# A streaming encoder layer on one core: the recurrence moved, in half chunks, beside the paired projection products, and the window it had taken away

## The chip, the cores and the metric

The kernel runs on one core of a Trainium2 chip. The metric is the device time of one execution in microseconds (us), the median of several runs. The engines are TensorE (PE; its weight loads are listed apart as PEld), VectorE (DVE), ScalarE (ACT), GpSimd (POOL) and the queue that issues every DMA (SP).

## The reference

One layer for 1152 tokens: 1024 of a prompt and 8 x 16 of samples that continue from caches. From `u`, the normalised input, one projection gives eleven blocks of 1024 columns. Three branches use them, and a gated sum merges them:

```python
q, k, v, g_a, x_r, g_b, q_m, g_c, g_m = split(u @ w_in)
A: o_a = diff_attention(q, k, v) * silu(g_a)        # 8 heads, samples see 512 cached tokens
B: x_c = conv_b + sum(xpad[:, j:j+T] * conv_w[j])   # causal, width 4
   r, i = sigmoid(x_c @ rg_wa + rg_ba), sigmoid(x_c @ rg_wx + rg_bx)   # 8 diagonal blocks of 128
   a = exp(-8 * r * softplus(-rg_lambda));  b = sqrt(1 - a*a) * (i * x_c)
   h[t] = a[t] * h[t-1] + b[t];   o_b = h * silu(g_b)
C: o_c = cross_attention(q_m, memory of 256 tokens, 4 heads) * silu(g_c)
m = sum_i sigmoid(g_m[i]) * (o_i @ w_branch[i]);  y = LayerNorm(alpha * u + m @ w_o)
```

## The kernel before

All large products are made in three TensorE passes over a high and a low part (`mm3`, L142), and everything is held transposed: 128 channels on the partitions, the 1152 tokens along the free axis. `uhi` and `ulo` (8 channel blocks x 1152 tokens) are the moving operand of every projection and, later, of every merge: they hold `u` first and then one branch output after the other.

A **chunk** is 128 output columns of a weight matrix. `units_for` (L457) makes it in three **units** of 384 tokens, each of 24 matmuls, and loads the weights two chunks ahead. `gm_units` (L478) makes a chunk of merge gate `g_m` (a tanh on ACT, then a store to `d_gm`). `m_units(i, e)` (L488) makes chunk `e` of the merge of branch `i` (A is 0, B 1, C 2): it loads the gate (`gmr`) and, except for the first branch, the running sum (`mr`), combines them on DVE and stores the sum to `d_m`.

The body runs **windows** one after the other (L1404), each with its own SBUF pool and its own PSUM banks:

- a (L526): prompt self-attention with its own chunks, then one chunk of `g_m`
- s (L800): sample self-attention, with 6 chunks of `g_m` (18 units) put between its steps
- p (L1070): sums and differences of quarters of `u` (`piece`, L1076), with 3 chunks of `g_m`. A last set of five pieces overwrites one quarter of `uhi`/`ulo`
- g (L1145): the other 46 chunks of the projection, in 23 pairs (`jobs`)
- b (L1300): the recurrence of branch B, with A's merge (24 units) as filling
- c (L704): prompt cross-attention, with 9 units of B's merge
- x (L951): sample cross-attention, with the other 15 units of B's merge

C's merge, the output product and the final LayerNorm follow. Two functions put a branch output back into `uhi`/`ulo`: `o_get` (L509) loads it from `d_oT`, and `o_put` (L514) splits it with a cast on ACT and a subtraction on DVE.

A **job** of window g makes two chunks with seven products of half the depth and half the tokens instead of eight. `step(i, j)` (L1238) is product `j` of job `i`: 24 matmuls of 288 tokens, two halves of 12. Three accumulators, X, Z and Y, of two PSUM banks each, rotate from job to job:

```python
mov = [B11, T3, 1, B21, 0, B22, 2]
role = ["X", "Z", "X", "Y", "X", "X", "Z"]
```

X takes products 0, 2, 4 and 5, and it is read out after each of them, so the readout of one half must be over before the next product's matmuls of that half. `g_prep(q + 3)` (L1113) makes the weights of a product three products ahead: on DVE the sums, then a cast on ACT and a subtraction on DVE. The banks of Z of one job are those of Y in the next. A job that makes `x_r` ends in the convolution (`Conv.done`, L1184: eight DVE instructions); one that makes a gate ends in a tanh on ACT and a product on DVE.

Window b takes the 8 channel blocks one after the other, in five steps for each: the gates of three stretches of 384 tokens (six groups of three matmuls, tanh on ACT), `rec1` (L1328: exponential, tanh and square root on ACT, a product on POOL, two on DVE), `rec2` (L1342: the scan over all 1152 tokens on DVE) and `rec3` (L1356). The split input `xhl` and the gate tile `t` have one buffer each. Its order is written out as

```python
wk.seq = [setup] + weave(fill[:20], at) + fill[20:23] + [lambda: put(0), fill[23], lambda: put(1), lambda: put(2)]
```

`weave` spreads one list evenly over another. This is the order in which instructions are asked for; a list scheduler then gives each engine its queue, in which an instruction that it reckons to be ready may stand ahead of one asked for earlier. On the chip every engine, and SP, works through its queue in order.

Of the kernel before, what the change touches and what calls it, by code (L numbers as in the profile page):

```python
# [18 lines left out]
D = 1024  # L19
# [15 lines left out]
GM_T = (1, 6, 3)  # L35
# [83 lines left out]
def body(tc, A):  # L119
# [355 lines left out]
    gmp = pool(left, "gmp", 4)  # L475
    gm_next = [0]

    def gm_units(stop=False):  # L478
# [3 lines left out]
        def ev(c, t):  # L482
            g = gmp.tile([128, TC], F32, name="gms", tag="gms")
            SC.activation(g, t, AF.Tanh, scale=0.5)
            SY.dma_start(d_gm[i][:, TC * c:TC * c + TC], g)
        return units_for(COL_GM + 128 * i, ev, stop=stop)

    def m_units(i, e, put=None, stop=False):  # L488
        x = {}

        def pre(c):
            x["g"] = gmp.tile([128, TC], F32, name="gmr", tag="gms")
            SY.dma_start(x["g"], d_gm[8 * i + e][:, TC * c:TC * c + TC])
            if i:
                x["m"] = gmp.tile([128, TC], F32, name="mr", tag="ms", bufs=3)
                SY.dma_start(x["m"], d_m[e][:, TC * c:TC * c + TC])

        def ev(c, t):
# [5 lines left out]
            if i:  # L504
                V.tensor_tensor(g, x["m"], g, OP.add)
# [12 lines left out]
    def gate_ev(G):  # L518
        def ev(c, t):
            g = gmp.tile([128, TC], F32, name="gts", tag="gms")  # L520
# [183 lines left out]
    def window_c():  # L704
# [88 lines left out]
        for e in range(3):  # L793
            fill += m_units(1, e)
# [5 lines left out]
    def window_s():  # L800
# [112 lines left out]
        def fin2(g):  # L913
# [10 lines left out]
            if g == 1:  # L924
                SY.dma_start(d_oT[0].rearrange("h p t -> p h t")[:, :, S:T], X["oT"])
# [25 lines left out]
    def window_x():  # L951
# [93 lines left out]
        for e in range(3, 8):  # L1045
            fill += m_units(1, e)
# [21 lines left out]


    def window_p():  # L1070
# [5 lines left out]
        def piece(c, n, last):  # L1076
            q = {}
            need = ((0, 1), (1, 1)) if last else ((0, 0), (0, 1), (1, 0), (1, 1))
            for k, t in need:
# [3 lines left out]
            if last:  # L1083
                sub(y[0], q[1, 1], q[0, 1])
                a = (slice(None), slice(0, 4), slice(TH + c, TH + c + n))
                split(uhi[a], ulo[a], y[0])
                return
# [6 lines left out]
        cs = [(128 * j, 128) for j in range(4)] + [(512, 64)]  # L1094
        fill = []
        for j in range(GM_T[2]):
            fill += gm_units(stop=j == GM_T[2] - 1)
        a = [lambda c=c: piece(*c, False) for c in cs]
        wk.seq = weave(fill, a) + [lambda: (g_load(0), g_load(1), g_prep(0))]
        wk.seq += [lambda c=c: piece(*c, True) for c in cs]  # L1100
# [12 lines left out]
    def g_prep(q):  # L1113
# [7 lines left out]
        elif j == 1:  # L1121
            a = tmp("s3")
            sub(a, quad(0, 0), quad(1, 0))
# [5 lines left out]
        elif j == 3:  # L1129
            a = quad(0, 1)  # L1130
# [405 lines left out]
```

## Time and profile before

| | us |
|---|---|
| median of 3 runs (2023.32 to 2025.5) | 2025.39 |
| the profiled execution | 2022.76 |
| its span, first to last instruction | 2021.0 |
| PE busy in the span | 1948.7 |
| DVE busy | 1229.9 |
| ACT busy | 851.1 |
| POOL busy | 104.6 |

The span is what the rows below divide; the profiled execution is 1.8 us longer than its span. PE's busy time is modelled, since matmuls overlap: two matmuls of 384 tokens are each listed with about 0.34 us, though in a row one starts every 0.174 us. So PE's real time is read from where instructions start, or from a run of equal ones, not from the busy column.

### The profile page before, as it was taken

To read this page: it belongs to the slowest core of one execution; us is meant where nothing else is said; L and a number is where in the kernel's file an instruction comes from. 1 tells how busy PE (TensorE), PEld (TensorE's weight loads), DVE (VectorE), ACT (ScalarE), POOL (GpSimd) and SP (SyncE) were. 2 spreads that over 40 slices of the span, in tenths; PEclk is the share of its full clock that TensorE was granted. 3 is DMA by queue.
4 is the path that set the end of the run, shared out by engine and by line. 5 is a ranking of instruction groups with operands and counts; after the bars stand their busy time and mean duration, and the time that the engine had idled before them with its cause. 6 is when DMAs were issued, how large, how long until landed. Compare 5 with 4: busy or idle time off the path is not lost.

```text
span 2021.0 us, 34019 instructions
## 1 busy us (share of the span) xinstructions
PE 1948.7 (96%) x13424; PEld 1827.6 (90%) x13424; DVE 1229.9 (61%) x2404; ACT 851.1 (42%) x1725; POOL 104.6 (5%) x178
## 2 busy tenths in 40 slices
PE   7999999999999999999999999999999499999998
PEld 7999999999999876799999999999999398889986
DVE  7731787667786444446554565555667675454397
ACT  5432566555665333333333333434666452232120
POOL 2100000000000011000000000000011101000000
PEclk9999999999999999999999999999999699999999
DMA  8753122211221487664223222333876486895332
GB/s 271 247 147 101 40 71 67 78 55 53 63 67 58 141 285 238 189 189 131 95 97 116 100 101 90 110 100 112 268 231 208 164 294 223 285 302 174 102 126 94
DMA packets 291487, 297.36 MB, mean 147 GB/s; under 512 B 17332, under 2 KB 255028, under 8 KB 291328
## 3 DMA queue, kind: packets, MB, share of 16 engines
q1 hardware_dynamic: 291328, 295.20, 45.6%
q8 instruction: 105, 1.72, 0.4%
q14 instruction: 54, 0.44, 0.1%
HBM read 209.54 MB, written 85.61 MB: 146 GB/s over the span
## 4 chain that ended last, share of the span: by engine, by line
PE 83%; DMA 5%; DVE 5%; ACT 3%; issue 2%; SPq 1%; POOL 0%; DVEq 0%; ACTq 0%; POOLq 0%
PE pj L140 39%; PE ba L1261 8%; PE bb L1261 8%; PE bc L1261 8%; PE sc L140 7%; PE o L140 5%; PE tr L641 2%; PE tr L855 1%; DMA ocr<-d_oT 1%; PE pv L140 1%; ACT K L567 1%; DMA uq<-d_u 1%; DVE t L1352 1%; PE tr L982 1%; DMA xc<-d_xc 1%
## 5 line engine op out<-in xcount | busy, mean ns | idle before, releaser
L140 PE MATMUL pj<-uhi,xh 128*128 128x384 f32 x1392 | 477.9, 343 | 2.1 <-DVE soT L921 1.5
L140 PE MATMUL pj<-uhi,xl 128*128 128x384 f32 x1392 | 474.4, 341 | 0.0
L140 PE MATMUL pj<-ulo,xh 128*128 128x384 f32 x1392 | 472.9, 340 | 0.6 <-DVE ulo L133 0.6
L140 PEld LDWEIGHTS pj<-uhi,xh 128*128 128x128 f32 x1392 | 263.1, 189 | 11.2 <-issue 9.1
L140 PEld LDWEIGHTS pj<-uhi,xl 128*128 128x128 f32 x1392 | 262.9, 189 | 7.1 <-issue 6.1
L140 PEld LDWEIGHTS pj<-ulo,xh 128*128 128x128 f32 x1392 | 263.0, 189 | 6.4 <-issue 5.3
L136 ACT CAST xh<-xr 128x512 fp32r<-128x512 f32 x150 | 90.0, 618 | 177.0 <-PE pj L140 103.8
L623 ACT ACTIVATE p<-p,sst 128x256 f32<-128x256 f32 (+6 forms) x128 | 100.6, 786 | 17.7 <-DVE sst L620 16.3
L140 PE MATMUL pj<-w,uhi 128*128 128x256 f32 x576 | 106.9, 285 | 0.5 <-ACT uhi L136 0.2
L133 DVE TENSOR_TENSOR xl<-xr,xh 128x512 fp32r<-128x512 f32 x116 | 78.9, 685 | 44.3 <-ACT xh L136 44.0
L140 PE MATMUL pj<-wo,mh 128*128 128x512 f32 x432 | 98.6, 390 | 0.4 <-ACT wo L136 0.4
L620 DVE CUSTOM_DVE_ANT_0 p<-sc,th 128x256 f32<-128x256 f32 (+6 forms) x128 | 96.5, 768 | 3.1 <-PE sc L140 2.0
L140 PEld LDWEIGHTS pj<-wo,mh 128*128 128x128 f32 x432 | 80.8, 188 | 17.9 <-ACT wo L136 1.1
L140 PE MATMUL sc<-K,Q 128*128 128x512 f32 (+4 forms) x384 | 94.5, 356 | 0.0
L140 PEld LDWEIGHTS pj<-w,uhi 128*128 128x128 f32 x576 | 90.5, 191 | 1.6 <-ACT uhi L136 0.9
L500 DVE SCALAR_TENSOR_TENSOR gmr<-gmr,pj 128x384 f32<-128x384 f32 x72 | 39.6, 550 | 81.0 <-PE pj L140 80.9
L140 PE MATMUL pj<-w,ulo 128*128 128x256 f32 x288 | 82.2, 286 | 1.7 <-DVE ulo L133 1.6
L140 PE MATMUL o<-v,wT 128*128 128x128 f32 x576 | 80.2, 278 | 0.0
L140 PEld LDWEIGHTS o<-v,wT 128*128 128x128 f32 x576 | 74.2, 192 | 3.4 <-ACT wT L169 1.5
L551 DVE SCALAR_TENSOR_TENSOR Q<-pj,Q 64x384 fp32r<-64x384 f32 (+1 forms) x48 | 24.5, 511 | 79.7 <-ACT Q L550 79.2
L140 PEld LDWEIGHTS sc<-K,Q 128*128 128x128 f32 x384 | 63.9, 189 | 3.8 <-DVE sst L620 1.5
L567 ACT CAST K<-kr 64x384 fp32r<-64x384 f32 (+1 forms) x96 | 45.7, 476 | 48.4 <-DVE kr L562 47.2
(314 smaller groups left out, 4055.2 us busy)
## 6 DMA issues: line engine op xcount, KB each, us to landing
xr<-in_w_in_dram SPq DMA_DIRECT2D x80, 512.0 KB, 4.0
ck<-in_cache_k_dram SPq DMA_DIRECT2D x32, 512.0 KB, 4.9
cv<-in_cache_v_dram SPq DMA_DIRECT2D x16, 1024.0 KB, 5.5
gmr<-d_gm SPq DMA_DIRECT2D x72, 192.0 KB, 3.3
xr<-in_w_branch_dram SPq DMA_DIRECT2D x24, 512.0 KB, 4.9
ocr<-d_oT SPq DMA_DIRECT2D x32, 384.0 KB, 5.0
d_m<-gmr SPq DMA_DIRECT2D x48, 192.0 KB, 3.3
mr<-d_m SPq DMA_DIRECT2D x48, 192.0 KB, 4.3
```

What stands on the lines that cost most here:

```text
L133: V.tensor_tensor(out, a, b, OP.subtract)
L136: SC.copy(hi, src)
L140: PE.matmul(out, a, b, start=start, stop=stop)
L500: V.scalar_tensor_tensor(g, g, 1.0, t, op0=OP.add, op1=OP.mult)
L551: V.scalar_tensor_tensor(q[b], t[a, :n], -1.0, raw(q[a]), op0=OP.mult, op1=OP.subtract)
L567: SC.copy(kh[b], kr[a, :n])
L620: V.tensor_tensor_reduce(s[:, :L].rearrange("p (a b) -> p a b", a=nb), ps[z][:, :nb, :w], X["th"][:, 896 - 128 * i:896 - 128 * i + L].rear ...
L623: SC.activation(s[:, :L], s[:, :L], AF.Exp, scale=-1.0, bias=st_[:, z, i:i + 1], accum_out=st_[:, 2 + z, i:i + 1])
L641: PE.transpose(t[:, 128 * j:128 * j + 128], X["w", h, i][:, 128 * k:128 * k + 128], ident)
L855: PE.transpose(t[:, 128 * j:128 * j + 128], X["ck", n, s // 2][:, j, 128 * (s % 2):128 * (s % 2) + 128], ident)
L982: PE.transpose(t[:, 256 * d + 128 * m:256 * d + 128 * m + 128], X["k", b][:, m, c:c + 128], ident)
L1261: PE.matmul(t, w[:, p, k, :], m[v][:, k, a], start=first and k == 0 and y == 0, stop=last and k == 3 and y == 2, skip_group_check=True)
```

## The change

The windows are now a, p, g, s, c, x; window b is gone.

- The recurrence runs in window g, in 16 halves (8 blocks x 2 halves of 576 tokens), seven steps each, woven between the products from job 8 to the last but one. The carry from one half to the next is the column `hc`. Its gates use two more PSUM banks (`tr`).
- Window s has B's merge (24 units) in place of 6 chunks of gates. Its output goes into `uhi`/`ulo` at once for the samples, and A's prompt output is loaded at its end.
- Window c has 12 units and window x the other 12 of A's merge.
- The 6 chunks of gates that were in window s are made in pairs: 26 jobs, 52 chunks. The eight jobs with a convolution come first, one after the other.
- In a job, the product into Y is now the second and the one that reads the overwritten quarter the fourth. The five pieces that overwrite that quarter are asked for at the start of window g.
- The pool of the gate tiles (`gmp`) is closed during window g and opened again, as `gmq`, behind it.

```diff
-GM_T = (1, 6, 3)
+GM_T = (1, 3)
     def m_units(i, e, put=None, stop=False):
+        more = i != 1
...
-            if i:
+            if more:
...
     def window_c():
-        for e in range(3):
-            fill += m_units(1, e)
+        for e in range(4):
+            fill += m_units(0, e)
...
     def window_s():
-        for _ in range(GM_T[1]):
-            fill += gm_units()
-        end = weave(fill[-6:], [lambda: None, fin, lambda: None, lambda: (fin2(0), fin2(1))])
-        wk.seq = weave(at, fill[:-6]) + end
+        for e in range(8):
+            fill += m_units(1, e)
...
+        f = [fill[0], fill[3], fill[1], fill[2], fill[4], fill[5]] + fill[6:]
+        wk.seq = weave(at, f[:-6]) + [outs, f[-6], fin, f[-5], lambda: (fin2(0), fin2(1)), f[-4],
+                                      lambda: [get(k, 0) for k in range(0, 8, 2)],
+                                      f[-3], f[-2], lambda: put(0), f[-1], lambda: put(1),
+                                      lambda: put(2), lambda: split(uhi[:, :, S:T], ulo[:, :, S:T], X["oT"])]
...
     def window_x():
-        for e in range(3, 8):
-            fill += m_units(1, e)
+        for e in range(4, 8):
+            fill += m_units(0, e)
...
     def g_prep(q):
         elif j == 1:
-            a = tmp("s3")
-            sub(a, quad(0, 0), quad(1, 0))
+            a = quad(0, 1)
...
         elif j == 3:
-            a = quad(0, 1)
+            a = tmp("s3")
+            sub(a, quad(0, 0), quad(1, 0))
...
     def window_g():
-        wk = Window(tc, "wkg", {"ba": 2, "bb": 2, "bc": 2})
+        wk = Window(tc, "wkg", {"ba": 2, "bb": 2, "bc": 2, "tr": 2})
         def start():
             g_prep(1)
             g_prep(2)
+            for c, n in TCS:
+                t = wk.tile([128, 2, 4, 128], F32, name="uz", tag="go", bufs=2)[:, :, :, :n]
+                for k in range(2):
+                    SY.dma_start(t[:, k], d_u[4 * k:4 * k + 4, :, TH + c:TH + c + n].rearrange("k p t -> p k t"))
+                sub(t[:, 1], t[:, 1], t[:, 0])
+                a = (slice(None), slice(0, 4), slice(TH + c, TH + c + n))
+                split(uhi[a], ulo[a], t[:, 1])
...
+        def rload(n, e):
...
+            X["xc"] = wk.tile([128, TH], F32, name="rc", tag="rc", bufs=2)
+            SY.dma_start(X["xc"], d_xc[n][:, c])
+            X["G"] = wk.tile([128, TH], F32, name="rG", tag="rG")
+            SY.dma_start(X["G"], d_gb[n][:, c])
+        def rsplit(n, e):
...
+            X["xhl"] = wk.tile([128, 2, TH], F32R, name="rx", tag="xcv")
+            split(X["xhl"][:, 0], X["xhl"][:, 1], X["xc"])
+            X["t"] = wk.tile([128, 2, TH], F32, name="rt", tag="xp")
+        def gates(n, h):
+            a = slice(TQ * h, TQ * h + TQ)
+            for z in range(2):
+                t = bank("tr")
+                mm3(t[:, :TQ], [y[:, z, :] for y in X["w", n]], [X["xhl"][:, y, a] for y in range(2)], True, True)
+                SC.activation(X["t"][:, z, a], t[:, :TQ], AF.Tanh, scale=0.5, bias=hb[:, n, z:z + 1])
+        def rec1(n):
...
+            SC.activation(a, r, AF.Exp, scale=q, bias=q)
+            SC.activation(r, r, AF.Tanh, scale=s, bias=s)
+            V.scalar_tensor_tensor(xc, i, 1.0, xc, op0=OP.add, op1=OP.mult)
+            GP.tensor_tensor(i, a, a, OP.mult)
+            V.scalar_tensor_tensor(r, i, 1.0, r, op0=OP.add, op1=OP.mult)
+            SC.activation(r, r, AF.Sqrt)
...
         jobs = weave(oth, jobs)
+        jobs = [(COL_XR + 128 * n, COL_GB + 128 * n, Conv(n), Plain(f_gate(d_gb[n]))) for n in range(8)] + jobs
-        mov = [B11, T3, 1, B21, 0, B22, 2]
-        role = ["X", "Z", "X", "Y", "X", "X", "Z"]
+        mov = [B11, B21, 1, T3, 0, B22, 2]
+        role = ["X", "Y", "X", "Z", "X", "X", "Z"]
...
+        m = 1 + 7 * 8
         end = wk.seq[-3:]
+        wk.seq = wk.seq[:m] + weave(wk.seq[m:-7], rec) + wk.seq[-7:-3]
+        wk.seq += [end[0], lambda: (w_load(na[0]), w_load(na[0] + 1)),
+                   lambda: o_b([(0, 0), (2, 0), (4, 0), (6, 0)]), end[1], lambda: o_b([(0, 1)]), end[2],
+                   lambda: [w_split(na[0] + j // 2, j % 2) for j in range(4)],
+                   lambda: o_b([(2, 1), (4, 1), (6, 1)])]
-    def window_b():
...
-    wins = [window_a(), window_s(), window_p(), window_g(), window_b(), window_c(), window_x()]
+    wins = [window_a(), window_p(), window_g()]
+    na.append(len(order))
+    wins += [window_s(), window_c(), window_x()]
```

## Rows read from the trace of the kernel before

**Rows 1.** The page's first part: busy us, share of the span, instructions.

```profile
PE 1948.7 (96%) x13424; PEld 1827.6 (90%) x13424; DVE 1229.9 (61%) x2404; ACT 851.1 (42%) x1725; POOL 104.6 (5%) x178
```

**Rows 2.** Busy us by stretch: windows s, g, c and x (granted clock, DMA share, GB/s).

```profile
690.00:881.00 191.00, 187.32 (x1695) 140.99 (x1694) 69.93 (x156) 59.01 (x137) 18.33 (x96) 1.00 0.72 228
926.00:1426.00 500.00, 500.00 (x3767) 500.00 (x3767) 291.23 (x466) 192.68 (x378) 11.22 (x30) 1.00 0.32 104
1612.00:1704.00 92.00, 91.39 (x566) 83.43 (x567) 70.54 (x107) 42.57 (x105) 0.00 (x0) 1.00 0.73 249
1704.00:1812.00 108.00, 100.73 (x774) 85.81 (x773) 52.90 (x113) 31.03 (x62) 5.55 (x2) 1.00 0.88 302
```

**Rows 3.** Busy us by stretch from the last job to window c: PE PEld DVE ACT POOL.

```profile
1434.80:1574.00 139.20, 130.02 (x715) 126.26 (x714) 97.94 (x122) 92.71 (x120) 16.01 (x19) 0.97 0.75 240
1574.00:1603.00 29.00, 4.96 (x17) 2.96 (x15) 18.25 (x18) 14.86 (x17) 4.91 (x6) 0.50 0.25 82
1603.00:1620.40 17.40, 16.85 (x84) 16.25 (x84) 7.50 (x11) 4.29 (x7) 0.00 (x0) 0.87 0.74 268
```

**Rows 4.** The same, of merge units alone (tile pj): PE PEld DVE ACT.

```profile
1434.80:1574.00 139.20, 104.15 (x576) 100.52 (x576) 13.13 (x24) 0.00 (x0) 0.97 0.75 240
...
1603.00:1620.40 17.40, 16.64 (x80) 15.88 (x80) 1.66 (x3) 0.00 (x0) 0.87 0.74 268
```

**Rows 5.** PE's waits from 1434.8 to 1620: us in total, times, longest.

```profile
PE tr L140 <- ACT t L1325: 11.2, 2, 10.2
PE tr L1366 <- POOL hlast L1354: 10.9, 1, 10.9
```

**Rows 6.** The chain that ended last: start, us; one unit, two products of window g.

```profile
687.09 4.18 PE pj L140 x24
...
986.63 3.18 PE bc L1261 x24
...
992.99 3.18 PE bb L1261 x24
```

**Rows 7.** Busy us by stretch, the first two jobs of window g.

```profile
917.20:945.10 27.90, 24.11 (x170) 23.87 (x169) 18.02 (x32) 10.18 (x22) 1.48 (x4) 0.94 0.31 91
945.10:967.40 22.30, 22.30 (x171) 22.30 (x170) 14.83 (x24) 8.14 (x16) 0.55 (x2) 1.00 0.36 127
```

**Rows 8.** DVE's timeline behind a convolution job: start, us.

```profile
988.03 4.46 DVE L1195 SCALAR_TENSOR_TENSOR xcv<-xp,small,xcv 128x1024 f32<-128x1024 f32 x6
992.41 0.68 DVE L133 TENSOR_TENSOR xh<-s,xh 128x512 fp32r<-128x512 f32 x1
993.01 0.81 DVE L1276 TENSOR_TENSOR go<-bc,gx 128x288 f32<-128x288 f32 x2
```

**Rows 9.** The recurrence's instructions by line and form: busy us, mean ns, idle before.

```profile
L1325 ACT ACTIVATE t<-tr,hb 128x384 f32<-128x384 f32 x48 | 25.0, 579 | 11.3 <-PE tr L140 7.1 <-DMA d_oT<-t 2.4 <-DVE xc L133 1.4
L1352 DVE TENSOR_TENSOR_SCAN t<-a,xc 128x1152 f32<-128x1152 f32 x8 | 20.4, 2555 | 0.2
L1337 POOL TENSOR_TENSOR t<-a 128x1152 f32<-128x1152 f32 x8 | 17.4, 2170 | 129.6 <-ACT a L1334 68.9 <-DVE xc L1336 60.7
L1338 DVE SCALAR_TENSOR_TENSOR t<-t,t 128x1152 f32<-128x1152 f32 x8 | 10.8, 1355 | 12.3 <-POOL t L1337 12.3
L1339 ACT ACT_TABLE_LOAD x8 | 10.3, 1283 | 0.1
```

**Rows 10.** ACT's timeline around one square root: start, us, wait before.

```profile
1480.79 1.17 ACT L1339 ACTIVATE t<-t 128x1152 f32<-128x1152 f32 x1 [3.76 <-DVE a L1351]
1483.49 1.28 ACT L1325 ACT_TABLE_LOAD   x1 [1.53 <-DVE xc L1345]
1484.78 0.58 ACT L1325 ACTIVATE t<-tr,hb 128x384 f32<-128x384 f32 x1
```

**Rows 11.** All of PE's waits in window s: us in total, times, longest.

```profile
PE tr L855 <- DMA ck<-in_cache_k_dram: 1.8, 1, 1.8
PE pj L140 <- DVE soT L921: 1.5, 1, 1.5
```

More of the change, by code (lines that the diff above doesn't have):

```diff
@@ L503, in ev @@
                 return
-            if i:
+            if more:
                 V.tensor_tensor(g, x["m"], g, OP.add)
@@ L1067, in tail_s @@
         return t[:, S:T].rearrange("p (b i) -> p b i", b=NB)
+    TCS = [(128 * j, 128) for j in range(4)] + [(512, 64)]
     def window_p():
@@ L1092, in piece @@
                 split(ut[j][0][:, :, c:c + n], ut[j][1][:, :, c:c + n], y[j])
-        cs = [(128 * j, 128) for j in range(4)] + [(512, 64)]
         fill = []
[L1096 to L1100, printed above, removed]
+        for j in range(GM_T[1]):
+            fill += gm_units(stop=j == GM_T[1] - 1)
+        a = [lambda c=c: piece(*c) for c in TCS] + [lambda: (g_load(0), g_load(1))]
+        wk.seq = weave(fill, a) + [lambda: g_prep(0)]
         return wk
@@ L1252, in step @@
             m = ut[m] if isinstance(m, int) else m
-            first, last = j in (0, 1, 3), j in (3, 5, 6)
+            first, last = j in (0, 1, 3), j in (1, 5, 6)
             x1, z7, x2 = X["x"]
@@ new lines, in o_b @@
+        def o_b(ps):
+            for k, e in ps:
+                X["o"] = 1 - X.get("o", 1)
+                t = wk.tile([128, 2, TH], F32, name="ocr", tag=("xp", "xcv")[X["o"]])
+                a = slice(TH * e, TH * e + TH)
+                SY.dma_start(t, d_oT[1][k:k + 2, :, a].rearrange("k p t -> p k t"))
+                split(uhi[:, k:k + 2, a], ulo[:, k:k + 2, a], t)
+        rec = []
+        for n in range(8):
+            for e in range(2):
+                rec += [lambda n=n, e=e: rload(n, e), lambda n=n, e=e: rsplit(n, e), lambda n=n: gates(n, 0),
+                        lambda n=n: gates(n, 1), lambda n=n: rec1(n), lambda n=n, e=e: rec2(n, e),
+                        lambda n=n, e=e: rec3(n, e)]
@@ L1411, in body, with gms @@
     w_split(0, 1)
-    for w in wins[:2]:
-        w.run(cur)
-    stT = ExitStack()
-    utp = stT.enter_context(tc.tile_pool(name="ut", bufs=1, side="right", reuse_waits="tile"))
-    ut = [[utp.tile([128, 4, TH], F32R, name=f"ut{j}{z}") for z in range(2)] for j in range(3)]
-    for w in wins[2:4]:
-        w.run(cur)
+    def gms():
+        st = ExitStack()
+        gq_[0] = pool(st, "gmp", 4)
+        return st
+    with gms():
+        wins[0].run(cur)
+        stT = ExitStack()
+        utp = stT.enter_context(tc.tile_pool(name="ut", bufs=1, side="right", reuse_waits="tile"))
+        ut = [[utp.tile([128, 4, TH], F32R, name=f"ut{j}{z}") for z in range(2)] for j in range(3)]
+        wins[1].run(cur)
+    wins[2].run(cur)
     stT.close()
-    for w in wins[4:]:
+    gq_[0] = pool(left, "gmq", 4)
+    for w in wins[3:]:
         w.run(cur)
```

206 lines of the change are left out of this document (78 added, 128 removed).

## Prediction

> **What bounds the kernel now.** I read the page's first part, then a table of stretches cut at the windows, then PE's waits in each window, and last the chain of waits, for what one unit costs. The first part says PE [rows 1], but the busy column overstates PE, so the question in every window is whether PE's queue ran without a hole. In window g it did: 500 us busy of 500, with DVE at 58% and ACT at 39% [rows 2]. In window s PE waited for anybody only twice, 3.3 us in all [rows 11], so that window is as long as PE's work and each unit added costs its full time. One unit of 24 matmuls takes 4.18 us and one product of 24 matmuls 3.18 us [rows 6], so a matmul of 384 tokens costs 0.174 us and one of 288 0.1325 us.
>
> The hole is window b. From the end of the last job to the end of its last gate transposes (1434.8 to 1603.0) 168.2 us pass. PE had 24 units to make in it (576 matmuls [rows 4]), 24 x 4.18 = 100.3 us, and 144 gate matmuls, 25.1 us, and eight small transposes, which I put at 1 us: 126.4 us. So 41.8 us are lost. Most are lost at the end: all 576 are done before 1574, and from 1574 to 1603 PE is busy for 5 of 29 us [rows 3], waiting 10.2 us for a gate's tanh and 10.9 us for the last scan [rows 5]. The granted clock falls there to 0.50, the lower of the two levels, and the 84 instructions behind it take 17.4 us [rows 3]: 80 unit matmuls [rows 4] are worth 13.9 us and four transposes about 0.4, so 3.1 us are the clock. **Window b costs 45 us more than its PE work.**
>
> **What the change takes away.** With window b gone its units stand elsewhere: s has 24 instead of 18, c 12 instead of 9, x 12 instead of 15, which makes 48 where 66 were, and the 18 that are missing are the six gate chunks that are now pairs. Those cost 18 x 4.18 = 75.2 us, and three jobs of seven products cost 3 x 7 x 3.18 = 66.8 us: **-8.4 us**. The gates are 192 matmuls of 288 tokens for 144 of 384: 25.4 for 25.1 us, **+0.3**. The 45 us go if the recurrence fits beside the products: **-45**.
>
> Does it fit? Window g becomes 26 x 7 x 3.18 + 25.4 = 604 us. DVE has 291 us of work there now [rows 2]; three more jobs at about a 23rd of it (12.7 us) add 38, and the recurrence has the same elements in halves: the scans 20.4 us and five like L1338's 10.8 [rows 9], 74 us. That is 403 of 604 us, 67%. ACT has 193 us and gets 25 for the jobs, 25.0 for the tanhs of the gates [rows 9], about 37 for four passes (a cast, exponential, tanh and square root at 1.17 us for 1152 tokens [rows 10], so 8 x 4 x 1.17), and table loads. The square root needs another table than exponential and tanh, so each half needs two loads of 1283 ns [rows 9]: 32 x 1.28 = 41 us. Together 321 of 604, 53%. Neither becomes the bound by its sum.
>
> The Trainium skill ("ScalarE: Activation LUTs", section "What ACT_TABLE_LOAD costs") speaks against the halves: it puts a switch at about 1283 ns for the load and 1380 ns for a drain, 2.66 us, by which the 32 switches are 85 us and ACT's sum 365, still 60%. The trace has the load at 1283 ns, but behind it the tanh starts at 1484.78, 0.01 us after the load ends [rows 10]: no drain shows, and the measurement decides.
>
> **Where PE can be held up in window g.** PE's queue is in order, and X and Y have deadlines.
>
> Products 4 and 5 both write X. The first half of 4 is done 1.6 us after it begins, product 5 wants that bank 3.18 us after, and a readout takes about 0.4 us (two in 0.81 [rows 8]), so DVE may come about 1.1 us late. ACT, which reads out products 0 and 2, has one product more in between, some 4.4 us. A recurrence half has a scan of 1.28 us (half of 2555 ns) with 0.7 us ahead of it on DVE, and on ACT two loads, three passes of 0.6 us and the wait of the square root. When one of these falls on a readout, PE stands for the rest. In the order the halves take 7.4 steps each against 7 products, so they drift across the jobs, and only some meet products 4 or, on ACT, 0 and 2. Bounds: nothing, up to 2 us for each of 16 halves, 32 us. I take 0.4 us each, nearer to nothing because DVE idles a third of the time and ACT half: **+6**.
>
> Y is now the second product of a job, and its banks were Z's, whose last readout is of product 6: only one product lies between, where it was three. Behind a convolution that readout is late. In the one shown, product 6 starts at 986.6 and the next job's second product at 993.0 [rows 6], but DVE is in the convolution until 992.4, then in a weight's subtraction, and begins the two readouts at 993.01 [rows 8], about 0.5 us too late for the first. Before, ACT had emptied the banks that this product wanted. Bounds for eight such jobs: nothing, if the subtraction slips behind, or 2 us each, if two more preparations go first, 16 us. I take 0.6 each: **+5**.
>
> **The borders.** The first job took 27.9 us where the next took 22.3 [rows 7]: 5.6 us, in which the second product waited for the five pieces. Now the fourth needs them, two products (6.4 us) later. I leave 1 us: **-4.6**. Bounds -5.6 and +5.6, the wait doubled, because two buffers now serve all five pieces. The two waits of window s [rows 11] lay on its border to a and to p; I count them off, **-3.3**. The new borders g to s and s to c each load, split and fill again with ready units as cover: nothing to 21 us (the two long waits at the tail of window b, 10.2 and 10.9 us [rows 5]), I take **+5** for both, nearer to the 3.3 of window s. Window x loses 12.5 us of units while its loads stay; it already moves 302 GB/s at 88% of the DMA engines [rows 2]: nothing to those 12.5 us, **+2**, since PE's share there is still 93%.
>
> **Sum.** -45 - 8.4 + 0.3 + 6 + 5 - 4.6 - 3.3 + 5 + 2 = -43 us. The span of 2021.0 becomes 1978, the profiled execution of 2022.8 some 1980. The median of the runs is 2.6 us above that execution, so I forecast 2025.4 - 43 = **1982 us**.
>
> **Rivals.**
>
> *The halves block ACT and DVE.* ACT is in order too: behind a table load the square root waited 3.76 us for DVE [rows 10], and whatever stands behind it waits as well, the readouts of products 0 and 2 and the casts of the weights. With half the size that wait may be 1.9 us; with two loads, two passes and that, ACT is closed for some 5.6 us, over the 4.4 it may be late. If every half costs PE 2 us instead of 0.4: 16 x 2 - 6 = 26 more, **2008 us**. Against it: three products of lead for the weights, 9.5 us. By the Trainium skill's drain (same page and section) two more times 1.38 us would stand in each burst, an estimate of 44 us over 16 halves if none of it hid, and this rival would be the likelier; the trace, which shows no such drain, speaks against that. Chance 0.18.
>
> *A tail again.* At the end of window s, or between g and s, the units run out before the loads and splits arrive, as in window b. One such tail of 21 us (10.2 + 10.9 [rows 5]) in place of the 5 gives **1998 us**. For it: the scheduler let all 24 units of window b run ahead. Against it: in s and x, where units stand between steps of another kind of work, PE hardly waited. Chance 0.11.
>
> *Slower.* The products lose their rhythm: PE stands at the readouts for the whole of each half's burst. Without the recurrence's term the change is worth 49 us, so it decides from 49 / 16 = 3.1 us for each half on. If the 3.76 us and the table load of 1.28 fall on PE whole, 16 x 5.0 = 80 us replace the 6, and the time is **2056 us**. For it: window b's own gates waited on ACT for 11.2 us in two places [rows 5]. Against it: the sums of 67% and 53%. Chance 0.07.
>
> *Everything is hidden*, with no new stall: -45 - 8.4 + 0.3 - 5.6 - 3.3 = -62, **1963 us**. Chance 0.02.
>
> **How the numbers follow.** My forecast holds 0.62, with its own range of 1968 to 1996 from half of the open terms. Differences under 0.2%, 4 us, can't be told from no change here. The forecast, the hidden case and the tail are faster; of the blocked halves I give 0.15 to faster and 0.03 to the same. So faster 0.90, same 0.03, slower 0.07. The range of 1964 to 2008 leaves out the slower case, about half of the blocked halves, and the hidden case: 0.18.
>
> **What would show it.** Window g should be about 615 us long, with jobs 9 to 25 near 22.3 us plus 1.5 us of gates, and the first seven borders between convolutions half a microsecond longer; the table loads should number 32 more or less there. No stretch behind the first microseconds should show the clock at 0.5. Windows s, c and x should take about 216, 105 and 98 us. Wrong would be: PE waiting in window g for a readout (`go` on DVE, `gx` on ACT) for tens of microseconds, or a hole at the end of s.

## The result, and the profile after

| | us |
|---|---|
| kernel after, median of 4 runs (1970.69 to 1976.63) | 1974.51 |
| kernel before, median of 4 runs beside it | 2025.45 |
| ratio, 95% interval | 0.9747 [0.9729, 0.9765] |
| the profiled execution after, its span | 1973.74, 1971.6 |

The kernel is 51 us faster; the forecast was 43 us faster, 1982, with a range of 1964 to 2008. The span fell from 2021.0 to 1971.6, 49.4 us, and that is the difference that the terms below have to explain.

The page's first part after, beside [rows 1]:

```profile
PE 1915.4 (97%) x13544; PEld 1814.3 (92%) x13544; DVE 1256.6 (64%) x2522; ACT 891.1 (45%) x1825; POOL 104.6 (5%) x186
```

DVE and ACT have more to do than before, PE about as many instructions. PE's idle time fell from 72.3 to 56.2 us, and its busy time, which overstates it, by 33.3 us; which work and which waits went has to be read from the stretches. Busy us by stretch after (PE, PEld, DVE, ACT, POOL, then granted clock, DMA share, GB/s), to be read against [rows 2, 3, 7]: the first job of g, the second, the other six with a convolution, jobs 9 to 25, the last job, the border from g to s, the rest of s, c, and x:

```profile
726.30:754.40 28.10, 23.81 (x169) 22.48 (x169) 16.08 (x28) 10.41 (x23) 0.00 (x0) 1.00 0.53 139
754.40:777.10 22.70, 22.53 (x170) 22.29 (x169) 18.17 (x31) 9.04 (x20) 2.37 (x6) 1.00 0.43 138
777.10:912.40 135.30, 135.30 (x1011) 134.07 (x1010) 95.97 (x163) 51.03 (x108) 8.44 (x24) 1.00 0.30 100
912.40:1318.40 406.00, 405.46 (x3049) 404.13 (x3049) 273.66 (x456) 258.57 (x457) 22.44 (x32) 1.00 0.41 130
1318.40:1340.80 22.40, 22.40 (x171) 22.31 (x169) 14.45 (x19) 15.05 (x23) 0.00 (x0) 1.00 0.85 265
1340.80:1361.90 21.10, 10.63 (x51) 9.68 (x49) 8.53 (x14) 6.17 (x8) 1.79 (x10) 0.87 0.87 267
1361.90:1563.10 201.20, 195.14 (x1858) 168.22 (x1859) 96.94 (x199) 62.34 (x137) 16.21 (x86) 0.98 0.85 272
1563.10:1665.10 102.00, 100.95 (x618) 92.22 (x619) 70.06 (x108) 42.44 (x105) 0.00 (x0) 1.00 0.70 236
1665.10:1762.30 97.20, 90.61 (x712) 76.06 (x711) 47.53 (x104) 28.14 (x58) 5.55 (x2) 0.98 0.85 295
```

Three things are to be seen. Jobs 9 to 25, beside which nearly the whole recurrence runs, take 406.0 us: 17 x 22.26 us of products and 25.4 us of gates are 403.8, so all 16 halves together cost 2.2 us at most. The row of the border, 1340.8 to 1361.9, has 48 unit matmuls worth 2 x 4.18 = 8.4 us in 21.1 us: here 12.7 us are lost. And window s as a whole (1340.8 to 1563.1) takes 222.3 us, though 12.7 us of it are lost. The unit matmuls in it (tile `pj`; PE, PEld, DVE, ACT), before and after:

```profile
690.00:881.00 191.00, 93.05 (x423) 70.46 (x422) 0.00 (x0) 8.82 (x18) 1.00 0.72 228
1340.80:1563.10 222.30, 123.81 (x626) 110.09 (x626) 14.34 (x26) 0.00 (x0) 0.97 0.85 271
```

These are 26 units, the window's own 24 and two of window c's that ran ahead. The 191.0 us of before [rows 2], 203 unit matmuls more (35.4 us) and the border's loss would make 239, so something in it became some 17 us cheaper, which I had not foreseen.

PE's waits in window g after (total us, times, longest):

```profile
PE bb L1356 <- ACT uhi L136: 1.3, 1, 1.3
PE ba L1356 <- DVE go L1371: 1.3, 1, 1.3
PE ba L1356 <- ACT gx L1363: 0.8, 1, 0.8
```

These three stand in the first 34 us of the window, while the pieces are made. There is no wait for a readout of "tens of microseconds", the sign of a wrong forecast. The four longest of PE's waits from 1325 to 1570, in window s and at its two ends:

```profile
PE tr L856 <- DMA ck<-in_cache_k_dram: 7.1, 1, 7.1
PE pj L140 <- ACT xh L136: 3.2, 1, 3.2
PE pj L140 <- DVE gmr L501: 2.2, 1, 2.2
PE tr L721 <- DMA mr<-d_kv: 2.1, 1, 2.1
```

The first two stand at the border from g, the third near the end of s, the last where c begins. ACT's timeline there tells how it comes about (start us, us, wait before):

```profile
1345.57 1.15 ACT L136 CAST uhi<-ocr 128x1152 fp32r<-128x1152 f32 x1 [3.09 <-DMA ocr<-d_oT]
1346.63 1.16 ACT L1229 ACTIVATE go<-go 128x1152 f32<-128x1152 f32 x1
1347.69 0.60 ACT L136 CAST xh<-xr 128x512 fp32r<-128x512 f32 x1
```

The cast at 1345.57 waits for one of the last pieces of B's output (`ocr`). Behind it stand the last gate's tanh and a cast of the next weights, which follow without a further wait; PE waits 3.2 us for that weight. A second cast of `ocr` follows at 1348.43, and the chain of waits carries on from it (start us, us):

```profile
1342.86 5.54 DMA ocr<-d_oT
...
1349.61 1.36 DVE ulo L133
1350.97 0.15 DVE qz L822
1351.12 0.21 SPq L811
...
1354.76 7.07 DMA ck<-in_cache_k_dram
```

The cast's subtraction on DVE (`ulo`) and a memset of window s behind it (`qz`) come first. Then SP asks for window s's bias, selection and sample tiles one after the other and only then, at 1354.76, for the first keys (`ck`), which land 7.1 us later. The two waits are 10.3 of the 12.7 us. Most of the rest is the clock, by stretch behind the first wait:

```profile
1344.96:1348.34 3.38, 0.17 (x1) 0.00 (x0) 1.37 (x2) 2.72 (x3) 0.00 (x0) 1.00 0.45 177
1348.34:1349.70 1.36, 1.25 (x5) 0.93 (x6) 0.76 (x2) 1.15 (x1) 0.00 (x0) 0.99 0.83 322
1349.70:1352.90 3.20, 3.20 (x11) 3.20 (x11) 2.77 (x7) 0.00 (x0) 0.00 (x0) 0.50 0.70 198
```

PE idles for 3.2 us, works again, and 1.4 us after it resumed the granted clock is at the lower level for 3.2 us: 11 matmuls, worth 1.9 us at the upper level, take 3.2. It is there twice more in window s, from the first matmul behind the 7.1 us without keys and, from 1551.0 to 1554.5 (granted 0.51), soon after the 2.2 us at the end of s:

```profile
1361.87:1366.75 4.88, 4.88 (x23) 3.25 (x23) 1.38 (x2) 1.17 (x2) 0.00 (x0) 0.50 1.08 360
```

By the two levels, half of these 8.4 us, some 4 us, is the most that they can have cost, an estimate.

Where window s wins its time is seen in PE's timeline at a score step (`sc<-kT,qz`, outputs of 32 partitions). Before:

```profile
727.08 0.61 PE L140 MATMUL sc<-kT,qz 128*32 128x264 f32 x2
727.62 0.66 PE L880 MATMUL tr<-ident,sp 128*128 128x128 f32 x4
...
728.75 0.63 PE L140 MATMUL sc<-kT,qz 128*32 128x264 f32 x2
729.32 0.44 PE L140 MATMUL pj<-ulo,xh 128*128 128x384 f32 x1
```

After:

```profile
1394.43 1.10 PE L140 MATMUL sc<-kT,qz 128*32 128x264 f32 x16
1395.46 0.33 PE L856 MATMUL tr<-ident,ck 128*128 128x128 f32 x1
```

From start to next start, two such matmuls take 0.54 and 0.57 us when other work stands on both sides, and 16 in a row take 1.03 us. Call those that start one behind the other, with no other matmul between, a run. Over the whole window the 256 records took 38.6 us in 80 runs before and 22.6 us in 24 runs after. That is 16 us, the largest term that the forecast did not have.

### The profile page after: what moved, and what is told of

Read it like the earlier page. It is cut to its first block, busy times and chain, and to the rows that moved or that the text cites. A ratio compares the mean times of both kernels' runs of the same rounds, so it can differ in the third digit from the quotient of the medians.

```text
span 1971.6 us, 34465 instructions
## 1 busy us (share of the span) xinstructions
PE 1915.4 (97%) x13544; PEld 1814.3 (92%) x13544; DVE 1256.6 (64%) x2522; ACT 891.1 (45%) x1825; POOL 104.6 (5%) x186
## 4 chain that ended last, share of the span: by engine, by line
PE 84%; DMA 6%; DVE 4%; ACT 4%; issue 1%; SPq 1%; DVEq 0%; ACTq 0%
PE pj L140 39%; PE ba L1356 9%; PE bb L1356 9%; PE bc L1356 9%; PE sc L140 6%; PE o L140 5%; PE tr L642 2%; DMA ocr<-d_oT 2%; PE tr L856 2%; PE pv L140 1%; PE tr L140 1%; ACT K L568 1%; PE tr L1007 1%; DVE w L259 1%; DVE ulo L133 1%
## 5 line engine op out<-in xcount | busy, mean ns | idle before, releaser
L140 PE MATMUL pj<-uhi,xh 128*128 128x384 f32 x1248 | 430.0, 345 | 5.4 <-ACT xh L136 3.2
L140 PE MATMUL pj<-uhi,xl 128*128 128x384 f32 x1248 | 424.4, 340 | 0.1
L140 PE MATMUL pj<-ulo,xh 128*128 128x384 f32 x1248 | 424.0, 340 | 0.0
L140 PEld LDWEIGHTS pj<-uhi,xh 128*128 128x128 f32 x1248 | 236.5, 190 | 8.6 <-ACT xh L136 3.5
L140 PEld LDWEIGHTS pj<-ulo,xh 128*128 128x128 f32 x1248 | 236.6, 190 | 2.1 <-issue 1.6
L140 PEld LDWEIGHTS pj<-uhi,xl 128*128 128x128 f32 x1248 | 236.1, 189 | 2.1 <-DVE xl L133 0.4
L133 DVE TENSOR_TENSOR xl<-xr,xh 128x512 fp32r<-128x512 f32 x106 | 72.0, 686 | 23.0 <-ACT xh L136 22.6
```

What stands on the lines that cost most here:

```text
L133: V.tensor_tensor(out, a, b, OP.subtract)
L140: PE.matmul(out, a, b, start=start, stop=stop)
```

## Experiments

### Six gate chunks as units again

```diff
-GM_T = (1, 3)
+GM_T = (1, 9)
```

> The changed kernel, with the six gate chunks made singly again (18 units in window p, 23 jobs in window g; the recurrence then has 14 jobs less one to run beside, not 17). Theory of the terms: 18 x 4.18 - 3 x 22.26 = 8.4 us more, about 1983 us, with window g some 67 us shorter and window p 75 us longer. Rival, that the paired chunks bring nothing because jobs beside the recurrence are held up: within 3 us of 1974.5. Rival, that 17 jobs are needed to hide the recurrence: over 1990, with the loss in window g.

Measured: 1991.27 us, ratio 0.982 [0.9803, 0.9836]; the span is 18.2 us longer than after (the median 16.8), where the arithmetic of the forecast gives 8.4. By stretch: windows a and p are 73.8 us longer (six chunks of 12.3), window g 62.3 us shorter and not 66.8, because 14 jobs instead of 17 now carry the recurrence and take 23.85 to 25.21 us each. That is 11.5 us net. Window s is 4.6 us longer; its wait for the first keys grew from 7.1 to 15.3. The windows c and x add 2.5 us. So the pairs are worth more than their matmuls: the exchange itself 73.8 - 66.8 = 7.0 us, and the jobs give the recurrence room. The time is that of the second rival, over 1990, but only 4.5 us of the loss lie in window g.

### Before, with 24 units beside the sample attention

```diff
-GM_T = (1, 6, 3)
+GM_T = (1, 8, 1)
```

> The kernel before, with two of the three gate chunks of window p moved to window s: 24 units there instead of 18, 3 in p instead of 9; the same work in all. Theory that the matmuls of window s cost less when more units stand between its steps (in the changed kernel the 256 score matmuls take 22.6 us of PE's time, before 38.7, because the list scheduler then keeps groups together): the score matmuls fall to some 23 to 28 us and window s is 10 to 16 us shorter than 24 units at full price would make it; window p, with less cover for its pieces, gives some or all of that back. Rival, that the order of windows or branch B's merge makes the difference, not the number of units: the score matmuls stay at 36 to 40 us and the time rises by what window p loses.

Measured: 2026.52 us, ratio 0.9996 [0.9986, 1.0006]. The score matmuls fell from 38.6 us in 80 runs to 25.3 us in 45, with nothing of the recurrence touched, and window g began 19.8 us earlier (897.5 instead of 917.3). But window p, left with one chunk, no longer covered its own pieces, and one wait in g's first job gave it all back:

```profile
PE bb L1261 <- ACT xh L136: 25.2, 1, 25.2
```

So the gain of the scores belongs to what is woven into window s, and comes without the recurrence's move; that the whole kernel could gain by it in this way is not shown, since the time is the same. The three chunks of window p were a cover that had its use.

### The recurrence left out, before and after

Before (of `rec1`, `rec2`, `rec3` and the gates nothing is left; a copy stands in their place):

```diff
...
-            at += [lambda n=n: gates(n, 0), lambda n=n: gates(n, 1),
-                   lambda n=n: (gates(n, 2), load(n + 1)), lambda n=n: rec1(n),
-                   lambda n=n: (rec2(n), rec3(n))]
+            at.append(lambda n=n: through(n))
...
```

> The kernel before without its recurrence: window b only copies the convolved rows through SBUF into branch B's output, and keeps its 24 units and the reload of branch outputs; gates, exponentials, scans are left out. Theory of the terms: the 41.8 us hole, the 3.1 us at the low clock and 25.1 us of gate matmuls go, 2025.4 becomes 1955 us. Rival, that the hole belongs to the reload of branch outputs and the start of window c rather than to the recurrence: only the gates go, 2000 us.

Measured: 1958.7 us, ratio 0.9673 [0.9641, 0.9704], 68.3 us under before. 25.1 us of that are gate matmuls, so 43 us are the hole that the forecast put at 45. The scores still took 38.6 us.

After, in the same way:

```diff
...
-                rec += [lambda n=n, e=e: rload(n, e), lambda n=n, e=e: rsplit(n, e), lambda n=n: gates(n, 0),
-                        lambda n=n: gates(n, 1), lambda n=n: rec1(n), lambda n=n, e=e: rec2(n, e),
-                        lambda n=n, e=e: rec3(n, e)]
+                rec += [lambda n=n, e=e: through(n, e)]
```

> The changed kernel without its recurrence, copied through in halves in the same way. Theory of the terms: 25.4 us of gate matmuls and some 2 us of stalls in window g go, 1974.5 becomes 1947 us, so the recurrence costs little beyond its matmuls. Rival, that the halves hold up the products or the border behind them by more: 1935 or less.

Measured: 1943.65 us, ratio 0.9584 [0.957, 0.9599], 30.9 us under after. Jobs 10 to 25 take 22.26 us each, to the hundredth. 25.4 us of the difference are gate matmuls again, so the recurrence costs the kernel after some 5.5 us beyond its PE work: 2.2 us at most in the jobs (without it job 9 still takes 23.57 us, 1.3 over the others), and window s with its border is 6.6 us shorter without it, of which the last job, 3.5 us longer, gives half back. A load that lasts 43 us beyond its PE work in a window of its own lasts 5.5 beside the products.

### The recurrence twice as dense

```diff
-        wk.seq = wk.seq[:m] + weave(wk.seq[m:-7], rec) + wk.seq[-7:-3]
+        wk.seq = wk.seq[:m] + weave(wk.seq[m:m + 63], rec) + wk.seq[m + 63:-3]
```

> The kernel after with all 112 steps of the recurrence woven into nine jobs (63 products) behind the convolutions, instead of into the sixteen and more that follow: about 1.8 steps behind each product instead of about one. The rival of the prediction that the halves hold up ScalarE and VectorE is tested where it is strongest. Theory A (half chunks are short enough that TensorE's four banks of evictions ride over them): the 25.4 us of gates move into the nine jobs, which take about 25.1 us each, the jobs behind them 22.26 us, stalls stay under 6 us in g, and the kernel stands at 1974 to 1979 us. Theory B (the prediction's rival: an engine that is nearly full holds up the evictions): VectorE and ScalarE would stand near 89 and 95% busy in those jobs, these grow to 27 to 29 us, and the kernel stands at 1990 to 2015 us.

Measured: 1993.53 us, ratio 0.9826 [0.9802, 0.985], 19 to 21 us slower than after. The profiled execution, 1999.65, is the longest of the four, so the losses below are rather large. By stretch, the nine jobs and the eight behind them, and the longest of PE's waits in the nine:

```profile
911.76:1165.02 253.26, 234.00 (x1701) 227.62 (x1700) 175.49 (x299) 181.06 (x311) 21.45 (x29) 0.99 0.42 133
1165.02:1343.90 178.88, 178.88 (x1352) 178.88 (x1351) 91.30 (x157) 77.89 (x147) 1.84 (x3) 1.00 0.34 111
```

```profile
PE tr L140 <- ACT rt L1273: 12.8, 11, 2.7
```

The nine jobs take 253.3 us where products and gates need 225.7: 27.5 us are lost, 1.7 us for each half instead of 0.14. So the rival of the blocked halves has a real mechanism and its size of 2 us each is about right, at this density. But not as I had put it: ACT is 71% busy in that stretch and DVE 69%, far from the 95 and 89 of my expectation, and the largest wait, 12.8 of the 27.5 us, is for the two gate banks (`tr`), which ACT empties in order behind whatever else stands in its queue. As far as the waits show it, PE is held by an engine's order, not by its load; all of PE's waits here come to 19 us, and the rest is not explained. With 7.4 products beside each half, as in the kernel after, the same bursts are covered; here it is 63 products for 16 halves.

### The old order of the products

```diff
-        mov = [B11, B21, 1, T3, 0, B22, 2]
-        role = ["X", "Y", "X", "Z", "X", "X", "Z"]
+        mov = [B11, T3, 1, B21, 0, B22, 2]
+        role = ["X", "Z", "X", "Y", "X", "X", "Z"]
```

(`g_prep` and the readouts go back with it.)

> The kernel after with the product order of before (Z product second, Y product fourth). Theory A (the new order has two small effects that nearly cancel): the eviction of the convolution's second product is back behind the fourth product, so the seven convolution jobs behind the second one lose their 0.27 us each and stand at 22.26 us again (-1.9 us); the second product of the first job needs the five pieces that are loaded at the start of g, so the first job grows from 28.1 us by one to two products' wait (+3 to +6 us). Sum 1976 us, range 1974 to 1979. Theory B (the order does not matter, the pieces are in time either way): the first job stays at 28 us and the kernel stands at 1972 to 1973 us. Theory C (the order is worth the whole of what the recurrence would otherwise stall): jobs 9 to 24 grow beyond 23.9 us and the kernel is above 1985 us.

Measured: 1969.49 us, ratio 0.9714 [0.9692, 0.9735]. The kernel after, timed again later, stood at 1972.26, 0.9729 [0.9713, 0.9745], so the times alone do not tell the two apart. The traces do: jobs 2 to 8 take 155.8 us, 22.26 each, instead of 158.0,

```profile
753.22:909.04 155.82, 155.82 (x1179) 155.82 (x1178) 116.44 (x193) 58.69 (x126) 9.63 (x29) 1.00 0.32 107
```

and the first job became shorter, not longer, 26.9 us. All three theories missed that. By the stretches the new order of the products costs some 3 us and brings nothing: PE waits for the pieces in the first job whichever product wants them first (`uhi` and `ulo`, 1.9 us here, 1.6 after). At the border to s the waits for a weight and for the keys, 3.2 and 7.1 us, became one for the keys, 13.7 us.

What is shown of the cost is the border of two convolution jobs in the kernel after. On DVE and on PE, around 893 us:

```profile
889.68 3.00 DVE L1224 SCALAR_TENSOR_TENSOR xcv<-xp,small,xcv 128x1024 f32<-128x1024 f32 x4
892.60 0.68 DVE L133 TENSOR_TENSOR xh<-s,xh 128x512 fp32r<-128x512 f32 x1
893.20 0.82 DVE L1371 TENSOR_TENSOR go<-bb,gx 128x288 f32<-128x288 f32 x2
```

```profile
893.02 0.85 PE L1356 MATMUL bc<-ut,xh 128*128 128x288 f32 x4
893.71 0.40 PE L1356 MATMUL bb<-uhi,xl 128*128 128x288 f32 x1
```

The readouts of `bb` begin behind the convolution and a weight's subtraction, as the forecast read it from before, and the second product waits for them. But the scheduler put four matmuls of the third product into the gap, so a border costs 0.27 us and not 0.6.

### A third buffer for the pieces

```diff
-            for c, n in TCS:
-                t = wk.tile([128, 2, 4, 128], F32, name="uz", tag="go", bufs=2)[:, :, :, :n]
+            for z, (c, n) in enumerate(TCS):
+                tag = ("go", "xcv", "go", "xcv", "go")[z]
+                t = wk.tile([128, 2, 4, 128], F32, name="uz", tag=tag, bufs=2 if tag == "go" else 1)[:, :, :, :n]
```

> The kernel after with a third buffer for the five pieces that are loaded at the start of g (two buffers in the kernel after). Theory A (the first job's 5.9 us of waits come from the pieces, whose loads wait for a buffer and whose casts stand ahead of the products' evictions on ScalarE): the first job falls from 28.1 to about 25 us and the kernel stands at 1971 to 1972 us. Theory B (the waits come from the work on the pieces, the subtractions and casts on VectorE and ScalarE, not from the buffers): the first job stays within 0.5 us of 28.1 us and the kernel at 1974 to 1975 us.

Measured: 1970.67 us, ratio 0.9717 [0.9695, 0.9739]; the first job takes 27.0 us, between the two theories. Alone it is 1.1 us of the 5.8 that the first job loses, and its time is not told apart from the kernel after.

### Five units ahead in window s

```diff
-        wk.seq = weave(at, f[:-6]) + [outs,
+        wk.seq = f[:5] + weave(at, f[5:-6]) + [outs,
```

> The kernel after with five of the 24 merge units of window s ahead of the attention's steps, without any step between them. Theory A (the border between g and s is lost to the attention's first load, which lands 21 us into the window, and to work of TensorE that is cut short by it): the five units keep TensorE busy over the load, the wait for it (7.1 us) falls under 2 us, and the kernel stands at 1966 to 1970 us; 19 woven units still leave the 256 score matmuls in long runs, 22 to 24 us. Theory B (the border is lost to the last piece of the output's operand, which arrives late and holds ScalarE and SyncE): the units ahead themselves wait for their gates, whose store and load stand behind that piece, the time moves from the load to their waits, and the kernel stands at 1972 to 1975 us. Rival on the scores: with units missing from the weave, pairs of score matmuls come back between the others, and their sum rises above 28 us.

Measured: 1966.58 us, ratio 0.9695 [0.9674, 0.9715]. PE's waits in s and at the start of c:

```profile
PE tr L721 <- DMA mr<-d_kv: 6.1, 1, 6.1
PE pj L140 <- ACT xh L136: 2.6, 1, 2.6
PE tr L856 <- DMA ck<-in_cache_k_dram: 1.5, 1, 1.5
```

The wait for the first keys fell from 7.1 to 1.5 us, as theory A had it, and window s from 222.3 to 214.2 us, although 4 us came back at its end as a longer wait for c's first tiles (6.1 for 2.1); c is some 2 us longer. The ratio's interval barely meets that of the kernel after timed again (0.9713 to 0.9745). The scores took 23.9 us in 29 runs: the rival on them falls.

### Three edits together, and loads put ahead

The first kernel has the old order, the third buffer and the five units ahead; the second has also these:

```diff
-        at = [lambda: (setup(), kload(0), qprep(0))]
+        at = [lambda: (kload(0), setup(), qprep(0))]
...
-        seq = [setup, lambda: qload(0)] + at[:8] + weave(at[8:], fill)
+        seq = [setup, lambda: qload(0)] + fill[:2] + at[:8] + weave(at[8:], fill[2:])
```

> The kernel after with three edits together: the product order of before, the third buffer for the pieces, and five merge units ahead in window s. Theory A (they act at three places and add): convolution jobs at 22.26 us (-2 us), first job 1 to 3 us shorter than 28.1 us, window s 8 us shorter and window c 2.5 us longer as with the units ahead alone; together 10 to 12 us below the kernel after. Theory B (they move one wait about): the ck wait at the start of s, which grew to 13.7 us with the old order, takes part of it back; 5 to 8 us below the kernel after, no better than the units ahead alone.

> The kernel before this one in the list (old order, third buffer, five units ahead) with two more edits of load order at window borders: window s asks for its first keys ahead of its bias, selection, query, key and gate loads, and window c has two of its units ahead of its first eight steps. Theory A (the borders are lost to what stands ahead in SP's queue): the ck wait is under 1 us and the mr wait at the start of c, 6.1 us with the units ahead, under 2 us; another 4 to 6 us less than the kernel with three edits. Theory B (the borders are lost to DMA throughput, about 270 GB/s with the 16 engines near 0.9 busy there): what is asked for earlier only delays the rest, and the time stays within 2 us of the three edits.

With them ran the kernel after once more:

> The kernel after, unchanged, beside the kernels of this call, so that differences of a few microseconds can be read between kernels timed on the same chip. Expected 1970 to 1975 us, ratio 0.973 to 0.975. If it stands at 1967 to 1969 us here, the 3 to 5 us that the kernel with the old product order and the one with a third buffer seemed to win are the chip's and not the edits'.

Measured: the kernel after 1972.26 us, 0.9729 [0.9713, 0.9745], as expected; three edits 1967.69, 0.9694 [0.9674, 0.9714]; with the loads ahead 1965.59, 0.9695 [0.968, 0.9709]. Window g became 4.7 us shorter than in the kernel after (609.8; first job 25.2), but s is 220.1 us, not 214.2. PE's waits at its start, with the three edits:

```profile
PE pj L140 <- DVE gmr L501: 6.3, 1, 6.3
```

The wait for the keys is gone, and another of the same size stands in its place: PE wants a bank that DVE has to read out (into a unit's gate tile, `gmr`), and on DVE that readout stands behind the subtraction of B's last piece, which waited for the cast of it, and behind six memsets of window s:

```profile
1345.28 1.36 DVE L133 TENSOR_TENSOR ulo<-ocr,uhi 128x1152 fp32r<-128x1152 f32 x1 [2.92 <-ACT uhi L136]
...
1348.77 0.95 DVE L501 SCALAR_TENSOR_TENSOR gmr<-gmr,pj 128x384 f32<-128x384 f32 x2
```

With the keys asked for first it is 6.8 us, and the wait at c's start still 5.4. So in both cases the time is that of theory B, with another wait than the first one named; that DMA throughput is the reason, as the second had it, is not shown. By the chain, the border's bound is the last half's way from the scan through DRAM into `uhi`; no run shortens that way, so this is read and not tested. The kernel with the loads ahead stands 6.7 us, 0.3%, below the kernel after that was timed beside it, with intervals that don't meet; that is no more than five units ahead gave alone.

### The order of the score matmuls

```diff
-            for e in range(2):
-                for s in range(4):
+            for s in range(4):
+                for e in range(2):
```

> The kernel after with the eight score matmuls of one sample job in another order: the two column halves of one head behind each other, instead of four heads of one half behind each other. Nothing else changes. The 256 records of these matmuls take 22.6 us in the kernel after (groups of four that start 7 ns apart, then 200 to 230 ns) and 38.6 us in before, where most stand in pairs of 0.40 us between the matmuls of the chunks. Theory A (matmuls of 32 columns on different quarters of the array run side by side, and what before lost was neighbours on other quarters): two neighbours now share a quarter, at most two run side by side, and the 256 records take 33 to 40 us although their runs stay long; the kernel is 8 to 16 us slower, 1982 to 1990 us. Theory B (what before lost was the change between chunk matmuls and score matmuls, so only the number of runs counts): 24 runs as before, 22 to 25 us, kernel within 2 us of the one after.

Measured: 1977.67 us, ratio 0.9751 [0.9736, 0.9765], an interval that overlaps that of the kernel after timed beside it (1972.26 us). The 256 records took 26.4 us in 24 runs, 3.8 us more than after. Of these, 1.4 us are one idle time of PE between two runs, and 1.0 us the first run, where the granted clock was 0.69 and 16 records took 2.04 us. A run of two alone takes 0.56 us in both kernels; the run of 16 shown here takes 1.05 us, the one above 1.03:

```profile
1395.59 1.12 PE L140 MATMUL sc<-kT,qz 128*32 128x264 f32 x16
1396.64 0.33 PE L856 MATMUL tr<-ident,ck 128*128 128x128 f32 x1
```

Theory A wanted 33 to 40 us and falls. Of theory B, the 24 runs came; the sum is 1.4 us above its 22 to 25, and the time 5.4 us above the kernel after where it had 2. Its thought fits the traces: what counts is how often PE goes over from whole-array work to these matmuls and back. For the scores alone the sum does not follow the runs evenly: 22.6 us at 24 runs, 23.9 at 29, 25.5 at 32 (three edits), 25.3 at 45, 38.6 at 80. But the value matmuls (`pv`) have 32 output partitions too, and runs that stand beside them cost less: of the 60 runs of two in the kernel before, the 38 with other matmuls on both sides took 0.56 us each, while 14 that had `pv` on both sides took 0.15. Counted together with `pv`, the sum follows the runs: 40.8 us at 27 (after), 42.1 at 32 (five units ahead), 43.8 at 34 (24 units before), 43.7 at 35 (three edits), 58.0 at 63 (before), so 17.2 us in 36 runs, 0.48 us each. The Trainium skill ("TensorEngine Tiling (Array Packing)", section "Key Properties") says that a change of the tiling mode drains TensorE, and these runs agree with it. Why the scheduler left 80 runs before and 24 after is not shown beyond what is woven in.

## Why the prediction was right

The direction and the mechanism were right, the sum was 8 us short in the median and 6 in the span. Term by term:

| term | forecast | measured | from |
|---|---|---|---|
| the hole of window b | -45 | -43 to -45 | recurrence left out of before |
| six chunks as pairs | -8.4 | -7.0 | pairs undone: 73.8 for 66.8 |
| gates of 288 tokens | +0.3 | +0.3 | same count of matmuls |
| stalls of the halves in g | +6 | +2.2 at most | jobs 9 to 25 |
| borders of convolution jobs | +5 | +2.1 | jobs 2 to 8, 158.0 for 155.8 |
| first job of g | -4.6 | +0.2 | 28.1 us, before 27.9 |
| the two waits of old window s | -3.3 | -3.3 | not there any more |
| borders g to s, s to c, and the end of s | +5 | +17 | 12.7 + 2.1 + 2.2 |
| window x | +2 | about 0 | 10.8 us shorter, with 63 unit matmuls (11.0 us) less |
| scores in window s | none | -16 | 38.6 to 22.6 us |

**The hole.** The step that carried the forecast held: the time was the recurrence's, and its steps run beside the products nearly free. Window g came out at 614.5 us, forecast about 615; jobs 9 to 25 at 23.9 us each, forecast 22.3 + 1.5; s, c and x together at 421.5, forecast 419 (222.3, 102.0 and 97.2 for 216, 105 and 98; two of c's units, 8.4 us, ran in s). DVE was busy for 418 and ACT for 344 of the 614.5 us, 68 and 56%, where the forecast had 403 and 321, 67 and 53%.

**The stalls.** 0.14 us for a half, not 0.4. The dense kernel shows that the forecast's worry was real and at what density it comes due.

**The table loads** are the 32 that were counted, 16 of them for the square root; the other 16 in window g stand before a tanh (8 at L1229, 4 at L1273, 4 at L1237). The instructions of the square root's line (first and last start in us) show no idle time between a load and its activation: the first load starts at 934.4, lasts 1283 ns, and the first square root starts at 935.7.

```profile
L1286 ACT ACT_TABLE_LOAD  x16: 1283/1283/1283, 934.4 to 1312.9; - x16
L1286 ACT ACTIVATE rt<-rt x16: 684/686/688, 935.7 to 1314.2; 128x576 f32<-128x576 f32 x16
```

Nor did ACT idle ahead of the loads: 0.3 us before these 16 together, 0.1 before each of the other groups. The drain of 1380 ns that the Trainium skill counts with each switch ("ScalarE: Activation LUTs", section "What ACT_TABLE_LOAD costs"), weighed in the forecast, does not show here either.

**The first job** is the step that failed in sign. The forecast read the 5.6 us of before as a wait for the five pieces. PE's only wait there was 3.8 us, for the cast of the second product's weight, whose subtraction stood on DVE behind those of the pieces; some 1.2 us more were the clock, 17 matmuls in 3.4 us, worth 2.25:

```profile
PE bb L1261 <- ACT xh L136: 3.8, 1, 3.8
924.90:928.30 3.40, 3.40 (x17) 3.40 (x16) 3.12 (x6) 1.29 (x3) 0.00 (x0) 0.51 0.00 0
```

So to want the pieces two products later did not take the loss away: after, two buffers serve five pieces one behind the other, and their casts stand in ACT's queue ahead of readouts. With a third buffer and the old order together the job fell to 25.2 us.

**The borders** were mis-sized three times over: 5 us forecast, 17 measured. The rival "a tail again" named the place and had 21 us for it. The late thing was not the units but the last half of B's output, and everything queued behind its cast on ACT and behind it on SP. The sign "no stretch at clock 0.5" was wrong with it, for 3.2 us, and again for 4.9 us behind the wait for keys and some 3.4 us at the end of s.

**What was missing** is the scores' -16 us. The forecast counted window s by its units and took the attention's own matmuls for constant. It made up for the borders, 12 us more than forecast, so that the total came out better than the sum of what was foreseen; that the two errors nearly cancel is luck. The measured terms add to between -47 and -50 us, and up to 4 us less with the two later stretches at the lower clock; the span fell by 49.4. They come from several kernels, so they need not add up to the last microsecond.

## What to carry to other kernels

A chain of small dependent steps that holds a window of its own is best put beside a long stream of products, thinly: with 7.4 products beside each half it cost 2 us, twice as dense 27, with ACT at 71% and DVE at 69% busy. Where the moved work ends, look at what is behind its last piece in each queue: an in-order cast that waits for a load holds every later one, and curing one such wait shows the next. And when units are woven between small matmuls, count how often the engine goes over between the two kinds: their price is in the runs, not in the number.

## What the runs showed of the hardware

Matmuls with 32 output partitions between whole-array matmuls cost about 0.27 us a record in twos (0.54 to 0.57 us) and 0.064 us a record in a run of 16 (1.03 us). A run of such matmuls, scores and values together, cost some 0.48 us beyond its records (17.2 us for 36 runs). Behind an idle time of PE of 3.2 us the granted clock was still 0.99 for the first 1.4 us of new work, and 0.50 for the 3.2 us after that; behind one of 7.1 us it was 0.50 from the first matmul on, for 4.9 us.
